# Moving the weight tiles of a decoder layer by 128 bytes and splitting its 512-column gate and up matmuls into 256-column ones

## The chip, the cores and the metric

The kernel runs on one core of a Trainium2 chip. The metric is the time of the program on the device, in microseconds; less is better. Before the change the runs took 1199.06 to 1200.92 us, median 1200.54. One further execution was profiled; it took 1200.04 us.

## The reference, cut to what matters

One decoder layer over 256 tokens of width 2048, in float32. An input projection feeds two groups of heads (a recurrent one, RWKV-7, and a latent attention), their outputs go through an output projection, and a gated MLP follows. The change touches the dense products around them; the core of the MLP is

```python
h = rms_norm(x, ffn_norm_g[l])
gate = h @ w_gate                       # 2048 x 5632
gate = causal_depthwise_conv(gate, width 3) + conv_b
x = x + (silu(gate) * (h @ w_up)) @ w_down
```

The input projection is `rms_norm(x) @ w_in`, 2048 by 4448; the latent attention adds `w_uq`, `w_ukv`, and `w_out` is 2048 by 2048. A row's normalising factor commutes with a product, so the kernel applies it after the product, when it evicts the result.

## The kernel before, in words

**Split products.** Every dense product is made of three float32r products, which together come near float32: a float32 matrix W is split into hi (rounded to float32r) and lo (the rest), an activation likewise, and the kernel sums hi·hi, hi·lo and lo·hi. `piece` (L125) loads 512 KB of weights into a tile `raw`, ScalarE writes `hi` (L133), VectorE writes `lo` (L134). There are three buffers each of `raw`, `hi` and `lo`, of 4 KB in a partition.

**Three ways to order a product.** In `prod_b` and `prod_c` the weights stand still in TensorE (one 128 by 128 block per load) and the activations stream past. An activation block holds hi and lo side by side, 2 times 256 tokens.

- `prod_b` (L162, used by the FFN's gate and up products alone) streams hi and lo together, 512 columns past a block of W's hi (L165), into a whole 512-column PSUM accumulator; then 256 columns past each block of W's lo (L168). The accumulator ends as two halves, which `joined` (L181) adds: a ScalarE copy (L182), a VectorE add (L183), a VectorE multiply by the row factors (L184).
- `prod_c` (L171, input projection and latent up projections) makes three matmuls of 256 columns into the same 256 columns: two on W's hi (L175, with the block loaded for each), one on W's lo (L178). `scaled` (L186) evicts it in one VectorE multiply (L187).
- `prod_a` (L190: value up projection, output projection, down projection) turns it round: activations stand still, 512 columns of weights stream past (L197 to L199).

**Stages.** Input projection with the activation tiles named x and most of the recurrent heads' work (to 272 us of the span), latent projections with tiles named cl and the heads' ends (to 342 us), output projection in two halves (to 462 us), then twice: gate and up products of a block of columns (24 and 20 blocks of 128 columns each; L964 to L988), and the down products on them (L993 to L1020). Each of the 44 blocks of gate and up takes two accumulators and four pieces of weights, a piece being 8 weight blocks: 176 pieces in all. The FFN's activation tiles, named z, are four buffers of the pool a8, the same four that x had. Queues are filled by a scheduler at build time; within an engine the order is then fixed.

**Where the tiles lie.** Pools and single tiles are laid out in a partition in the order in which they are first used: `pad` (8 floats), the four buffers of a8 (8 KB each), `pad2` (8 floats), and behind it everything else, the pools of hi, lo and of the 4 KB tiles (s4) among it. All buffers of a8, s4, hi and lo are whole multiples of 256 bytes long, and a matmul's operands start at multiples of 512 bytes in them. So two operands keep one distance modulo 256 whatever the buffer and the block. In the program as built, the a8 buffers start at byte 160 modulo 256, and s4, hi and lo at 96. Below, *distance* is the start of the streaming operand less the start of the standing one, modulo 256:

| products | streams | stands | columns | distance before |
|---|---|---|---|---|
| gate and up, L165 and L168 | z (a8) | hi, lo | 512, 256 | 64 |
| input projection, L175 and L178 | x (a8) | hi, lo | 256 | 64 |
| latent q and k, L175 and L178 | cl (s4) | hi, lo | 256 | 0 |
| down projection, L197 to L199 | hi, lo | hh, hl (s4) | 512 | 0 |
| output projection, first half | hi, lo | yhi, ylo (s4) | 512 | 0 |
| output projection, second half | hi, lo | yhi, ylo (a8) | 512 | 192 |
| last pieces of the down projection | wt (a8) | hh, hl (s4) | 512 | 64 |

Of the kernel before, what the change touches and what calls it, by code (L numbers as in the profile page):

```python
# [14 lines left out]
ALU = mybir.AluOpType  # L15
AX = mybir.AxisListType

P = 128
T = 256
# [35 lines left out]
def hybrid_layer(ctx: ExitStack, tc: tile.TileContext, a: dict, out: bass.AP):  # L55
    nc = tc.nc
    V, S, PE = nc.vector, nc.scalar, nc.tensor
# [8 lines left out]
    def nm(s):  # L66
        uid[0] += 1
        return f"{s}{uid[0]}"
# [3 lines left out]
    def s4(dt=F32, n="s4"):  # L72
        return sb.tile([P, 1024], dt, tag="s4", name=nm(n), bufs=NS4)
# [8 lines left out]
    def hl4(n):  # L82
        return a8(n).rearrange("p (k s) t -> p k s t", s=2)

    def t1(n, w=T, dt=F32):
        return sb.tile([P, 260], dt, tag="t1", name=nm(n), bufs=NT1)[:, :w]
# [7 lines left out]
    def mm(n="mm"):  # L94
        return ps.tile([P, 512], F32, tag="mm", name=nm(n), bufs=NMM)
# [4 lines left out]
    def at(n="at"):  # L100
        return ps.tile([P, 512], F32, tag="at", name=nm(n), bufs=NAT)

    def con(shape, n, dt=F32):
        return sb.tile(shape, dt, name=n, bufs=1)
# [2 lines left out]
    nc.gpsimd.memset(pad, 0.0)  # L107
    xT = a["xT"]
    xs_ = [hl4("x") for _ in range(4)]
    pad2 = con([P, 8], "pad2")  # L110
    nc.gpsimd.memset(pad2, 0.0)
    vec = con([P, NVEC], "vec")
    cst = con([P, NCST], "cst")
# [11 lines left out]
    def piece(src, dst=None, eng=None):  # L125
        raw = sb.tile([P, 1024], F32, tag="raw", name=nm("raw"), bufs=NRAW)
        last_w[0] = nc.sync.dma_start(raw, src).ins
        if dst is None:
            hi = sb.tile([P, 1024], F32R, tag="hi", name=nm("hi"), bufs=NHI)
            lo = sb.tile([P, 1024], F32R, tag="lo", name=nm("lo"), bufs=NLO)  # L130
        else:
            hi, lo = (dst.rearrange("p k t -> p (k t)")[:, q * 1024:(q + 1) * 1024] for q in range(2))
        S.copy(hi, raw)  # L133
        sub = (eng or V).tensor_tensor(lo, raw, hi.bitcast(F32), ALU.subtract).ins  # L134
        if eng is None:
            last_lo[0] = sub
        return hi, lo

    def xsplit(g):
        raw = s4(n="xraw").rearrange("p (k t) -> p k t", k=4)  # L140
        nc.sync.dma_start(raw, xT[:, g * 4:(g + 1) * 4, :])
        for j in range(4):
            k = g * 4 + j
            h = xs_[g][:, j, 0, :]
            S.activation(h, raw[:, j, :], AF.Copy, scale=vv("ag", k))
            last_x[0] = V.scalar_tensor_tensor(xs_[g][:, j, 1, :], raw[:, j, :], vv("ag", k),
                                               h.bitcast(F32), ALU.mult, ALU.subtract).ins
        return raw
# [5 lines left out]
    def flush(every=False):  # L154
        now = [f for n, f in pend if n == 0 or every]
        pend[:] = [(n - 1, f) for n, f in pend if n > 0 and not every]
        for f in now:
            f()
# [3 lines left out]
    def prod_b(acc, pieces, act, kt0, n, first, last):  # L162
        hi, lo = pieces
        for j in range(n):
            PE.matmul(acc, hi[:, j * P:(j + 1) * P], act(kt0 + j), start=first and j == 0, stop=False,  # L165
                      skip_group_check=True)
        for j in range(n):
            PE.matmul(acc[:, :T], lo[:, j * P:(j + 1) * P], act(kt0 + j)[:, 0, :], start=False,  # L168
                      stop=last and j == n - 1, skip_group_check=True)

    def prod_c(acc, pieces, act, kt0, n, first, last):  # L171
        hi, lo = pieces
        for j in range(n):
            for s in range(2):
                PE.matmul(acc[:, :T], hi[:, j * P:(j + 1) * P], act(kt0 + j)[:, s, :],  # L175
                          start=first and j == 0 and s == 0, stop=False)
        for j in range(n):
            PE.matmul(acc[:, :T], lo[:, j * P:(j + 1) * P], act(kt0 + j)[:, 0, :], start=False,  # L178
                      stop=last and j == n - 1)

    def joined(dst, acc, scale):  # L181
        S.copy(dst, acc[:, T:])  # L182
        V.tensor_tensor(dst, acc[:, :T], dst, ALU.add)  # L183
        V.tensor_tensor(dst, dst, scale, ALU.mult)  # L184

    def scaled(dst, acc, scale, rows=slice(0, P)):  # L186
        V.tensor_tensor(dst, acc[rows, :T], scale[rows], ALU.mult)  # L187


# [11 lines left out]
    x_hl = lambda k: xs_[k // 4][:, k % 4, :, :]  # L201

    def in_tile(i, pf=mm):
        acc = pf()
        for h in range(2):
            eng = nc.gpsimd if h and 17 <= i < 25 else None
            prod_c(acc, piece(a["win"][i, h], eng=eng), x_hl, h * 8, 8, h == 0, h == 1)
        flush()
        return acc

# [108 lines left out]
    acc0 = [mm(), mm(), at()]  # L319
    pcs = {}  # L320
# [10 lines left out]
    with tc.manual_schedule(engines={mybir.EngineType.SP}):  # L331
        for g in range(4):
            xsplit(g)
            if g == 0:
                nc.scalar.dma_start(cst, a["cst"])
            if g % 2 == 0:
                for i in range(2):
                    pcs[i, g // 2] = piece(a["win"][wt0[i], g // 2])
            for i in range(2):
                hl = tuple(u[:, (g % 2) * 512:(g % 2 + 1) * 512] for u in pcs[i, g // 2])  # L340
                prod_c(acc0[i], hl, x_hl, g * 4, 4, g == 0, g == 3)
        for h in range(2):
            prod_c(acc0[2], piece(a["win"][26, h]), x_hl, h * 8, 8, h == 0, h == 1)
        sums(0)
        kacc[0] = in_tile(1)
        dve0 = last_lo[0]
        sums(1)
        kacc[1] = in_tile(2, ch)
        rope_tables()
        lora = s4(n="lora")  # L350
        nc.sync.dma_start(lora, a["lora"])

    rsB = sb.tile([P, T], F32, tag="rsB", name="rsB", bufs=1)
# [30 lines left out]
    def shifted(acc, i, rows=slice(0, P), dst=None):  # L384
        h = t1("h", 257)
        nc.gpsimd.memset(h[rows, 0:1], 0.0)
        scaled(h[rows, 1:257], acc, rsB, rows)
        o = t1("sh") if dst is None else dst
        S.activation(o[rows], h[rows, 1:257], AF.Copy, scale=om_mu[rows, i:i + 1])
        V.scalar_tensor_tensor(o[rows], h[rows, 0:256], vv("mu", i, rows), o[rows], ALU.mult, ALU.add)  # L390
        return o
# [49 lines left out]

    acc = acc0[2]
    kraw, ksw = t1("kraw"), t1("ksw")
    scaled(kraw[0:64], acc, rsB, slice(0, 64))
    shifted(acc, 26, rows=slice(64, 96), dst=sg2)
    sigmoid_(sg2, slice(64, 96))
    nc.gpsimd.dma_start(kraw[64:128], kraw[0:64])
# [11 lines left out]
    for p in range(8):  # L459
        pp, g = p // 2, p % 2  # L460
# [3 lines left out]
        acc = kacc[p] if p in kacc else in_tile(1 + p)  # L464
# [45 lines left out]
    for p in range(8):  # L510
        pp, g = p // 2, p % 2
        acc = in_tile(9 + p)
# [254 lines left out]
    cl, rrs, rrB = [], [], []  # L767

    def latent(x, gname, post):
        c_ = [s4(F32R, "cl").rearrange("p (k s t) -> p k s t", k=2, s=2) for _ in range(2)]  # L770
        ssum = t2("css")
        for j in range(4):
            acc = in_tile(27 + x * 4 + j)
            cr = t2("cr")
            scaled(cr, acc, rsB)
            if j == 0:
                S.activation(ssum, cr, AF.Square)
            else:
                sq = t2("csq")
                S.activation(sq, cr, AF.Square)  # L780
                V.tensor_tensor(ssum, ssum, sq, ALU.add)
            h_, l_ = (c_[j // 2][:, j % 2, q, :] for q in range(2))
            S.activation(h_, cr, AF.Copy, scale=vv(gname, j))
            V.scalar_tensor_tensor(l_, cr, vv(gname, j), h_.bitcast(F32), ALU.mult, ALU.subtract)
        pss = at("pss")
        for tb in range(2):
            PE.matmul(pss[:, tb * 2:tb * 2 + 2], ssum[:, tb * P:(tb + 1) * P], ones[:, 0:2], start=True, stop=True)
        m = st("ssm", 2)
        V.tensor_copy(m, pss[:, 0:4:2])
        rr = con([P, 2], f"rr{x}")  # L790
        V.tensor_scalar(rr, rsqrt(m, 1.0 / 512, EPS, 2), post, None, ALU.mult)
        rb = con([P, T], f"rrB{x}")
        bcast(rr, rb, at, t2)
        rrs.append(rr)
        rrB.append(rb)
        cl.append(c_)
# [12 lines left out]
    def up_b(src, i, x, dsts):  # L809
        pcs = piece(src[i])  # L810
        for j in range(2):
            acc = mm()
            prod_c(acc, (pcs[0][:, j * 512:(j + 1) * 512], pcs[1][:, j * 512:(j + 1) * 512]),
                   lambda k: cl[x][k // 2][:, k % 2, :, :], 0, 4, True, True)
            scaled(dsts[j], acc, rrB[x])

    for i in range(4, 6):
        up_b(a["wuq"], i, 0, [qr[:, (i - 4) * 2 + j, :] for j in range(2)])
# [145 lines left out]
    for blk, nf in enumerate((24, 20)):  # L964
        hh = [s4(F32R, "hh").rearrange("p (k t) -> p k t", k=4) for _ in range(nf // 4)]
        hl = [s4(F32R, "hl").rearrange("p (k t) -> p k t", k=4) for _ in range(nf // 4)]
        for fi in range(nf):
            f = f0 + fi
            accs = []
            for gu in range(2):  # L970
                acc = mm()
# [24 lines left out]
        n = nf // 2  # L996
# [105 lines left out]
```

## Time and profile before

| | us |
|---|---|
| median of 3 runs | 1200.54 |
| the profiled execution | 1200.04 |
| its span, first to last instruction | 1198.3 |
| TensorE busy (PE) | 1164.2 |
| weight loads busy (PEld) | 1026.2 |
| VectorE busy (DVE) | 817.5 |
| ScalarE busy (ACT) | 582.9 |

The span is what the profile covers; 1.7 us of the execution lie around it. A matmul in the profile is two instructions, the load of the standing operand (PEld) and the matmul (PE), which overlap, and the recorded matmuls overlap each other too. So the pace of a stream of matmuls is read from the distance of two starts, not from the length of one. In the chain of waits, each line has the start in us, the length in us, the engine, the tile written, the line of the kernel, and how many were merged; along a stream of matmuls each of them is there from its own predecessor's end, so the length divided by the count is the pace.

### The profile page before, as it was taken

What the parts mean: (1) busy time and instruction counts of PE and PEld (TensorE: products, weight loads), DVE (VectorE), ACT (ScalarE), POOL (GpSimd) and SP (SyncE); (2) the same over time, 40 slices, a digit from 0 to 9 for tenths busy, and PEclk for the clock granted to TensorE, in tenths of its full rate; (3) what the DMA queues carried; (4) which work ended last, traced back from release to release, by engine and by line L of the source; (5) the groups of instructions that cost most, each with busy time, mean ns of one, the idle gap of its engine ahead of it and who ended that gap; (6) DMA issues with size and microseconds to landing.
All of it is one profiled execution on the core that took longest, in us unless ns stands there. A gap on an engine that the chain in (4) does not pass through costs nothing.

```text
span 1198.3 us, 19598 instructions
## 1 busy us (share of the span) xinstructions
PE 1164.2 (97%) x7633; PEld 1026.2 (86%) x7633; DVE 817.5 (68%) x1296; ACT 582.9 (49%) x883; POOL 77.3 (6%) x214
## 2 busy tenths in 40 slices
PE   7899998999999999999999999999999999999996
PEld 7899988998877888888888888888888888888885
DVE  6797549867986566777777775444577777775663
ACT  6674334433434455655555554333455555554542
POOL 1500232011110001000000000000000000000000
PEclk9999999989998999999999999999999999999999
DMA  8554454735233554655555555555655555566662
GB/s 325 169 156 162 133 155 140 226 106 181 89 124 124 184 182 165 205 193 187 189 191 190 194 193 187 189 197 190 204 191 191 187 191 191 193 219 213 202 217 81
DMA packets 71022, 215.90 MB, mean 180 GB/s; under 512 B 17616, under 2 KB 17872, under 8 KB 70928
## 3 DMA queue, kind: packets, MB, share of 16 engines
q1 hardware_dynamic: 69776, 211.84, 54.1%
q10 hardware_dynamic: 768, 2.05, 0.5%
q8 instruction: 60, 0.98, 0.3%
q0 software_dynamic: 384, 0.75, 0.3%
q14 instruction: 34, 0.28, 0.1%
HBM read 210.48 MB, written 3.41 MB: 179 GB/s over the span
## 4 chain that ended last, share of the span: by engine, by line
PE 91%; DVE 4%; DMA 2%; issue 1%; ACT 1%; SPq 1%; POOL 0%; ACTq 0%; POOLq 0%
PE mm L165 27%; PE mm L168 14%; PE mm L175 10%; PE mm L197 9%; PE mm L198 9%; PE mm L199 9%; PE mm L178 5%; PE pg L539 1%; PE px L689 1%; DVE Tq L596 1%; DMA xraw<-in_xT 1%; PE py L689 1%; DMA Lp<-dL 1%; DVE lo L134 0%; DMA xt<-in_x 0%
## 5 line engine op out<-in xcount | busy, mean ns | idle before, releaser
L134 DVE TENSOR_TENSOR lo<-raw,hi 128x1024 fp32r<-128x1024 f32 x368 | 450.3, 1224 | 274.5 <-ACT hi L133 271.0
L133 ACT CAST hi<-raw 128x1024 fp32r<-128x1024 f32 x376 | 394.7, 1050 | 477.0 <-issue 154.6
L165 PE MATMUL mm<-z,hi 128*128 128x512 f32 x1408 | 351.3, 392 | 0.0
L165 PEld LDWEIGHTS mm<-z,hi 128*128 128x128 f32 x1408 | 251.9, 188 | 43.7
L168 PEld LDWEIGHTS mm<-z,lo 128*128 128x128 f32 x1408 | 188.3, 188 | 14.5
L168 PE MATMUL mm<-z,lo 128*128 128x256 f32 x1408 | 191.6, 278 | 0.0
L175 PE MATMUL mm<-x,hi 128*128 128x256 f32 x1056 | 149.6, 289 | 11.6 <-ACT hi L133 8.2
L175 PEld LDWEIGHTS mm<-x,hi 128*128 128x128 f32 x1056 | 135.7, 194 | 14.5 <-ACT hi L133 8.2
L198 PE MATMUL mm<-lo,hh 128*128 128x512 f32 x336 | 130.7, 389 | 0.0
L199 PE MATMUL mm<-hi,hl 128*128 128x512 f32 x336 | 130.7, 389 | 0.0
L197 PE MATMUL mm<-hi,hh 128*128 128x512 f32 x336 | 119.7, 389 | 0.0
L178 PE MATMUL mm<-x,lo 128*128 128x256 f32 x528 | 77.2, 285 | 0.0
L199 PEld LDWEIGHTS mm<-hi,hl 128*128 128x128 f32 x336 | 63.1, 188 | 13.1
L197 PEld LDWEIGHTS mm<-hi,hh 128*128 128x128 f32 x336 | 63.1, 188 | 13.1
L198 PEld LDWEIGHTS mm<-lo,hh 128*128 128x128 f32 x336 | 63.1, 188 | 13.0
L178 PEld LDWEIGHTS mm<-x,lo 128*128 128x128 f32 x528 | 69.4, 193 | 0.1
L198 PE MATMUL mm<-lo,yhi 128*128 128x512 f32 x128 | 51.4, 402 | 0.0
L199 PE MATMUL mm<-hi,ylo 128*128 128x512 f32 x128 | 50.8, 397 | 0.0
L197 PE MATMUL mm<-hi,yhi 128*128 128x512 f32 x128 | 49.9, 409 | 0.0
L976 POOL MEMSET gt<- 128x2 f32 x44 | 4.3, 99 | 575.9 <-DVE hl L988 559.0
L199 PEld LDWEIGHTS mm<-hi,ylo 128*128 128x128 f32 x128 | 24.4, 190 | 5.3
L198 PEld LDWEIGHTS mm<-lo,yhi 128*128 128x128 f32 x128 | 24.4, 190 | 5.0
(277 smaller groups left out, 1111.0 us busy)
## 6 DMA issues: line engine op xcount, KB each, us to landing
raw<-in_wgu SPq DMA_DIRECT2D x176, 512.0 KB, 3.6
raw<-in_wdn SPq DMA_DIRECT2D x88, 512.0 KB, 4.2
raw<-in_win SPq DMA_DIRECT2D x70, 512.0 KB, 3.7
raw<-in_wout SPq DMA_DIRECT2D x32, 512.0 KB, 3.3
raw<-in_wuq SPq DMA_DIRECT2D x6, 512.0 KB, 3.3
xraw<-in_xT SPq DMA_DIRECT2D x4, 512.0 KB, 6.3
xt<-in_x SPq DMA_DIRECT2D x4, 512.0 KB, 6.9
raw<-in_wuv SPq DMA_DIRECT2D x4, 512.0 KB, 3.3
```

The costliest lines, as they stand in the source:

```text
L133: S.copy(hi, raw)
L134: sub = (eng or V).tensor_tensor(lo, raw, hi.bitcast(F32), ALU.subtract).ins
L165: PE.matmul(acc, hi[:, j * P:(j + 1) * P], act(kt0 + j), start=first and j == 0, stop=False, skip_group_check=True)
L168: PE.matmul(acc[:, :T], lo[:, j * P:(j + 1) * P], act(kt0 + j)[:, 0, :], start=False, stop=last and j == n - 1, skip_group_check=True)
L175: PE.matmul(acc[:, :T], hi[:, j * P:(j + 1) * P], act(kt0 + j)[:, s, :], start=first and j == 0 and s == 0, stop=False)
L178: PE.matmul(acc[:, :T], lo[:, j * P:(j + 1) * P], act(kt0 + j)[:, 0, :], start=False, stop=last and j == n - 1)
L197: PE.matmul(accs[tb], ah, wh, start=first and j == 0, stop=False)
L198: PE.matmul(accs[tb], ah, wl, start=False, stop=False)
L199: PE.matmul(accs[tb], al, wh, start=False, stop=last and j == n - 1)
L539: PE.matmul(pg[h][:, o:o + P], BK[pp][hs, gg, w * 2 + r, :, :], AR[pp][hs, gg, w * 2 + r, :, :], start=o == 0, stop=True, skip_group_check ...
L596: V.tensor_tensor(Tq[:, 0:n, i + 1:32], Tq[:, 0:n, i + 1:32], tv, ALU.add)
L689: PE.matmul(dst[HS[h], a_ * 64:(a_ + 1) * 64], lhsT, rhs, start=n == 0 and a_ == 0, stop=True, skip_group_check=True)
```

## The change

`pad2` gets 40 floats in place of 8, so everything behind it lies 128 bytes further on and the a8 buffers stay. `prod_c` takes the name `prod_b`, and the old `prod_b` goes; `scaled` takes the name `joined`, and the old three-step `joined` goes. So the FFN's gate and up products are made of three 256-column matmuls for each weight block, with one-step evictions, as the input projection's already were. All the other edits are these names.

```diff
-    pad2 = con([P, 8], "pad2")
+    pad2 = con([P, 40], "pad2")
...
     def prod_b(acc, pieces, act, kt0, n, first, last):
         hi, lo = pieces
         for j in range(n):
-            PE.matmul(acc, hi[:, j * P:(j + 1) * P], act(kt0 + j), start=first and j == 0, stop=False,
-                      skip_group_check=True)
-        for j in range(n):
-            PE.matmul(acc[:, :T], lo[:, j * P:(j + 1) * P], act(kt0 + j)[:, 0, :], start=False,
-                      stop=last and j == n - 1, skip_group_check=True)
-
-    def prod_c(acc, pieces, act, kt0, n, first, last):
-        hi, lo = pieces
-        for j in range(n):
             for s in range(2):
                 PE.matmul(acc[:, :T], hi[:, j * P:(j + 1) * P], act(kt0 + j)[:, s, :],
                           start=first and j == 0 and s == 0, stop=False)
...
-    def joined(dst, acc, scale):
-        S.copy(dst, acc[:, T:])
-        V.tensor_tensor(dst, acc[:, :T], dst, ALU.add)
-        V.tensor_tensor(dst, dst, scale, ALU.mult)
-
-    def scaled(dst, acc, scale, rows=slice(0, P)):
+    def joined(dst, acc, scale, rows=slice(0, P)):
         V.tensor_tensor(dst, acc[rows, :T], scale[rows], ALU.mult)
```

The distances become: gate and up 192, input projection 192, latent q and k 0, down projection 0, output projection 0 in the first half and 64 in the second, the last pieces of the down projection 192.

On TensorE, one accumulator of the FFN (two pieces) stood like this before, in the middle of the first 24 blocks; the names are accumulator, streaming tile, standing tile, and x4 is four in a row:

```order
L165 MATMUL mm_6037<-z_4913,hi_6040 128x512 x4
L165 MATMUL mm_6037<-z_4914,hi_6040 128x512 x4
L168 MATMUL mm_6037<-z_4913,lo_6041 128x256 x4
L168 MATMUL mm_6037<-z_4914,lo_6041 128x256 x4
L165 MATMUL mm_6037<-z_4915,hi_6062 128x512 x4
L165 MATMUL mm_6037<-z_4916,hi_6062 128x512 x4
L168 MATMUL mm_6037<-z_4915,lo_6063 128x256 x4
L168 MATMUL mm_6037<-z_4916,lo_6063 128x256 x4
```

With the change, the same place on TensorE:

```order
L166 MATMUL mm_6221<-z_4913,hi_6224 128x256 x8
L166 MATMUL mm_6221<-z_4914,hi_6224 128x256 x8
L169 MATMUL mm_6221<-z_4913,lo_6225 128x256 x4
L169 MATMUL mm_6221<-z_4914,lo_6225 128x256 x4
L166 MATMUL mm_6221<-z_4915,hi_6254 128x256 x8
L166 MATMUL mm_6221<-z_4916,hi_6254 128x256 x8
L169 MATMUL mm_6221<-z_4915,lo_6255 128x256 x4
L169 MATMUL mm_6221<-z_4916,lo_6255 128x256 x4
```

Each run of four 512-column matmuls is a run of eight 256-column ones now; the runs on lo stay. A piece has 24 matmuls and weight loads in place of 16; over the FFN that is 1408 of each more.

On VectorE, one block of the FFN before (gt and up are the evicted gate and up, cv the convolution, lo the split of the weights that come next):

```order
L183 TENSOR_TENSOR gt_7045<-mm_6955,gt_7045 128x256
L184 TENSOR_TENSOR gt_7045<-gt_7045,rs2B 128x256
L134 TENSOR_TENSOR lo_7088<-raw_7085,hi_7087 128x1024
L980 SCALAR_TENSOR_TENSOR cv_7050<-gt_7045,vec,cv_7050 128x256
L981 SCALAR_TENSOR_TENSOR cv_7050<-gt_7045,vec,cv_7050 128x256
L134 TENSOR_TENSOR lo_7111<-raw_7108,hi_7110 128x1024
L183 TENSOR_TENSOR up_7055<-mm_7000,up_7055 128x256
L184 TENSOR_TENSOR up_7055<-up_7055,rs2B 128x256
L985 TENSOR_TENSOR up_7055<-up_7055,cv_7050 128x256
L134 TENSOR_TENSOR lo_7133<-raw_7130,hi_7132 128x1024
L988 TENSOR_TENSOR hl_5347<-up_7055,hh_5341 128x256
```

With the change, the same block on VectorE:

```order
L174 TENSOR_TENSOR gt_7092<-mm_6970,rs2B 128x256
L134 TENSOR_TENSOR lo_7109<-raw_7106,hi_7108 128x1024
L967 SCALAR_TENSOR_TENSOR cv_7095<-gt_7092,vec,cv_7095 128x256
L968 SCALAR_TENSOR_TENSOR cv_7095<-gt_7092,vec,cv_7095 128x256
L134 TENSOR_TENSOR lo_7139<-raw_7136,hi_7138 128x1024
L174 TENSOR_TENSOR up_7100<-mm_7031,rs2B 128x256
L134 TENSOR_TENSOR lo_7170<-raw_7167,hi_7169 128x1024
L972 TENSOR_TENSOR up_7100<-up_7100,cv_7095 128x256
L134 TENSOR_TENSOR lo_7200<-raw_7197,hi_7199 128x1024
L975 TENSOR_TENSOR hl_5347<-up_7100,hh_5341 128x256
```

The add is gone from each of the two evictions, and ScalarE loses its two copies (L182) in the same way. Up to the start of the FFN the order on TensorE, VectorE and ScalarE is that of before, and SyncE's queue of transfers is the same throughout.

More of the change, by code (lines that the diff above doesn't have):

```diff
@@ L206, in in_tile @@
             eng = nc.gpsimd if h and 17 <= i < 25 else None
-            prod_c(acc, piece(a["win"][i, h], eng=eng), x_hl, h * 8, 8, h == 0, h == 1)
+            prod_b(acc, piece(a["win"][i, h], eng=eng), x_hl, h * 8, 8, h == 0, h == 1)
         flush()
@@ L340, in hybrid_layer @@
                 hl = tuple(u[:, (g % 2) * 512:(g % 2 + 1) * 512] for u in pcs[i, g // 2])
-                prod_c(acc0[i], hl, x_hl, g * 4, 4, g == 0, g == 3)
+                prod_b(acc0[i], hl, x_hl, g * 4, 4, g == 0, g == 3)
         for h in range(2):
-            prod_c(acc0[2], piece(a["win"][26, h]), x_hl, h * 8, 8, h == 0, h == 1)
+            prod_b(acc0[2], piece(a["win"][26, h]), x_hl, h * 8, 8, h == 0, h == 1)
         sums(0)
@@ L386, in shifted @@
         nc.gpsimd.memset(h[rows, 0:1], 0.0)
-        scaled(h[rows, 1:257], acc, rsB, rows)
+        joined(h[rows, 1:257], acc, rsB, rows)
         o = t1("sh") if dst is None else dst
@@ L443, in hybrid_layer @@
     kraw, ksw = t1("kraw"), t1("ksw")
-    scaled(kraw[0:64], acc, rsB, slice(0, 64))
+    joined(kraw[0:64], acc, rsB, slice(0, 64))
     shifted(acc, 26, rows=slice(64, 96), dst=sg2)
@@ L774, in latent @@
             cr = t2("cr")
-            scaled(cr, acc, rsB)
+            joined(cr, acc, rsB)
             if j == 0:
@@ L812, in up_b @@
             acc = mm()
-            prod_c(acc, (pcs[0][:, j * 512:(j + 1) * 512], pcs[1][:, j * 512:(j + 1) * 512]),
+            prod_b(acc, (pcs[0][:, j * 512:(j + 1) * 512], pcs[1][:, j * 512:(j + 1) * 512]),
                    lambda k: cl[x][k // 2][:, k % 2, :, :], 0, 4, True, True)
-            scaled(dsts[j], acc, rrB[x])
+            joined(dsts[j], acc, rrB[x])
     for i in range(4, 6):
```

## The prediction

> **What bounds the kernel now.** I read the page first, then the chain of waits in each stage. From the page: the span, the engines, and the chain by line.
>
> ```profile
> span 1198.3 us, 19598 instructions
> PE 1164.2 (97%) x7633; PEld 1026.2 (86%) x7633; DVE 817.5 (68%) x1296; ACT 582.9 (49%) x883; POOL 77.3 (6%) x214
> PE 91%; DVE 4%; DMA 2%; issue 1%; ACT 1%; SPq 1%; POOL 0%; ACTq 0%; POOLq 0%
> PE mm L165 27%; PE mm L168 14%; PE mm L175 10%; PE mm L197 9%; PE mm L198 9%; PE mm L199 9%; PE mm L178 5%; PE pg L539 1%; PE px L689 1%; DVE Tq L596 1%; DMA xraw<-in_xT 1%; PE py L689 1%; DMA Lp<-dL 1%; DVE lo L134 0%; DMA xt<-in_x 0%
> ```
>
> TensorE is the chain for 91% of the span, and 41% are the two lines of gate and up. Next the stretches: the FFN's first gate and up, and the input projection.
>
> ```profile
> 500.00:700.00 200.00, 200.00 (x1162) 176.09 (x1161) 146.39 (x218) 105.58 (x163) 1.89 (x19) 1.00 0.58 191
> 208.00:231.00 23.00, 23.00 (x198) 23.00 (x197) 20.27 (x42) 12.54 (x19) 0.00 (x0) 1.00 0.68 222
> ```
>
> Columns are the stretch, PE, PEld, DVE, ACT, POOL, granted clock, DMA share, GB/s. In the FFN, TensorE is busy all 200 us at full clock, VectorE 146, ScalarE 106, the DMA engines 0.58: nothing but TensorE limits it. So the pace of one matmul after another is what the change is worth, and the chain gives it. FFN, eight matmuls to a row:
>
> ```profile
> 479.24 0.91 PE mm L168 x8
> 480.14 1.83 PE mm L165 x8
> 481.97 0.94 PE mm L168 x8
> 482.92 1.83 PE mm L165 x8
> 484.75 0.91 PE mm L168 x8
> 485.66 1.83 PE mm L165 x8
> ```
>
> A 512-column matmul takes 1.83 / 8 = 229 ns. The 256-column ones come in two paces, in turn: 0.91 / 8 = 114 ns and 0.94 / 8 = 117.5 ns, same line, same shape, same distance of 64. The pace therefore isn't fixed by the shape. A piece is 2.74 or 2.77 us, 2.755 on average (479.24 to 481.97 and 481.97 to 484.75 are one of each).
>
> Now the same pace elsewhere. Input projection (256 columns, distance 64), then latent projections (256 columns, distance 0):
>
> ```profile
> 216.61 1.88 PE mm L175 x16
> 218.49 0.94 PE mm L178 x8
> 219.43 1.88 PE mm L175 x16
> 221.32 0.94 PE mm L178 x8
> ...
> 333.69 0.96 PE mm L175 x8
> 334.65 0.48 PE mm L178 x4
> ```
>
> The input projection takes 4.71 us for the 40 matmuls from 216.61 to 221.32, 117.8 ns each, and it stays there: the slower of the FFN's two paces, which I take at 117.8 too. The latent ones take (0.96 + 0.48) / 12 = 120 ns. And the 512-column ones, in the down projection (distance 0) and the output projection's second half (distance 192):
>
> ```profile
> 750.03 0.45 PE mm L197 x2
> ...
> 752.75 0.45 PE mm L197 x2
> ...
> 416.89 0.24 PE mm L197
> 417.12 0.23 PE mm L198
> 417.35 0.24 PE mm L199
> 417.59 0.23 PE mm L197
> 417.82 0.24 PE mm L198
> 418.06 0.23 PE mm L199
> 418.29 0.24 PE mm L197
> ```
>
> From 750.03 to 752.75 lie 12 matmuls: 226.7 ns each. From 416.89 to 418.29 lie six: 233.3 ns each. So with the streaming operand at distance 0, 64 and 192 from the standing one, 512 columns take 226.7, 229 and 233.3 ns; 256 columns take 120 at distance 0 and 114 or 117.8 at 64. Half of 226.7 is 113.3, which is the faster of the FFN's 256-column paces within the rows' rounding: I take it that 0.443 ns a column is the stream undisturbed (113.3 and 226.7), and the rest, 0 to 7 ns for each weight load, is the stream meeting the load of the next weights in the memory.
>
> The Trainium skill speaks against that reading: "TensorE: Matmul & The Clock Gate", section "Step-by-step: what each phase is for", has two independent read ports and says that loading the next weights takes no bandwidth from the running matmul. By that rule a shift of 128 bytes changes no pace. The rows of 114, 117.8 and 120 ns for one shape at one clock do not agree with it, unless something else than the address makes them; what it would give is the first rival below.
>
> **The change part by part.**
>
> Gate and up. Each of the 176 pieces has 24 matmuls of 256 columns in place of 8 of 512 and 8 of 256. Its price depends on the pace at distance 192 with 256 columns, which no row shows. The bounds: from below 113.3 ns, since no stream here goes under 0.443 ns a column; from above 120 ns by the slowest 256-column row, or, with what a 512-column load loses at 192 (233.3 − 226.7 = 6.6), 113.3 + 6.6 = 119.9, the same. Which value? The two widths order the distances in opposite ways: 512 columns lose 0 at distance 0, 2.3 at 64, 6.6 at 192, while 256 columns lose 6.7 at 0 and half as much at 64 (0 or 4.5). A 256-column matmul ends about when the load of the next weights does (PEld 23.00 of 23.00 us in the input projection, 176 of 200 in the FFN), so its stream and the load meet at another place in the pattern than in a 512-column one, and the losses fall along 0, 64 where those of the wide ones rise. Carried on to 192 that is no loss: 113.3 ns. This is a continuation over two points, not a proof, and the chance below says so. The sum: 24 × 113.3 = 2.720 us against 2.755, 35 ns a piece, 176 pieces, **−6.2 us**. At 120 ns it would be 2.880, +0.125 × 176 = +22.0 us.
>
> Input projection. The same matmuls on the same buffers, so the same pace: from 117.8 to 113.3, 4.5 ns each. Not all of them are on the path. In these rows stand the matmuls of L175 by stretch, and under them those of L178:
>
> ```profile
> 42.00:158.00 116.00, 70.22 (x496) 62.99 (x496) 0.99 0.47 146
> 195.00:272.00 77.00, 44.88 (x317) 40.98 (x315) 0.93 0.53 160
> 42.00:158.00 116.00, 34.26 (x241) 30.89 (x241) 0.99 0.47 146
> 195.00:272.00 77.00, 23.05 (x156) 21.20 (x157) 0.93 0.53 160
> ```
>
> Before 42 us the chain runs through transfers and the split of the weights, and from 158 to 195 us through the solve of the recurrent heads:
>
> ```profile
> 33.09 4.58 DMA raw<-in_win
> ...
> 167.12 6.14 DMA Lp<-dL
> 176.09 2.09 DVE Tq L596
> ```
>
> What is left on TensorE's path is 496 + 317 + 241 + 156 = 1210 matmuls: 1210 × 4.5 = **−5.4 us**. At 120 ns it is +2.7. What the rest gains there, TensorE waits for the transfers and the solve instead.
>
> Output projection, second half: its 192 matmuls (four column blocks, four pieces, twelve each) go from distance 192 to 64, so from 233.3 to 229 ns: 192 × 4.3 = **−0.8 us**. The last pieces of the down projection go the other way, 48 matmuls from 64 to 192: **+0.2 us**. Latent, first half and down projection keep distance 0 and their pace.
>
> Evictions. Of each of 88, ScalarE loses the copy and VectorE the add:
>
> ```profile
> L183 DVE TENSOR_TENSOR up<-mm,up 128x256 f32<-128x256 f32 x44 | 18.4, 418 | 0.0
> L182 ACT COPY gt<-mm 128x256 f32<-128x256 f32 x44 | 16.2, 367 | 0.0
> L165 PE MATMUL mm<-z,hi 128*128 128x512 f32 x1408 | 351.3, 392 | 0.0
> ```
>
> That is 88 × 0.42 = 37 us of VectorE and 88 × 0.36 = 32 us of ScalarE, all beside TensorE, which waits 0.0 us before L165: worth nothing now. They also leave more room for the splits of weights, so if a piece is 1% shorter, those still keep up: VectorE falls from 73% to about 66% of a piece, ScalarE from 53 to about 47%, and 191 GB/s become 193 with the DMA engines at 0.58. Were that cover gone, an eviction of 0.37 and 0.42 us and a multiply of that size, about 1.2 us, would stand open for each accumulator; there are three buffers for them, and two are in use.
>
> Sum: −6.2 − 5.4 − 0.8 + 0.2 = −12.2 us. The profiled execution's 1200.0 becomes 1187.8; it lies 0.5 under the median of the runs, so **1188 us**.
>
> **The rivals.**
>
> *The distance does nothing, and 256 columns cost what they cost in the input projection.* There the weight load is busy 23.00 of 23.00 us: the load of 128 columns and its hand-over would be the limit, not the stream, and 117.8 ns holds wherever every matmul is 256 wide. For it: the input projection's steady pace on the very buffers that z uses. Against: eight loads in a row at 114 ns in every other piece of the FFN. Time: 24 × 117.8 = 2.827 us a piece, +0.072 × 176 = +12.7 us, nothing elsewhere: 1213 us. It decides from 114.8 ns up (2.755 / 24), where the FFN gains nothing by the split. This is also what the Trainium skill's two ports would give.
>
> *Distance 192 costs 256 columns what it costs 512.* 6.6 ns a load, 120 ns: +22.0 in the FFN, +2.7 in the input projection, −0.6 from the two small groups: 1224 us. For it: the only rows at 192 are the slowest of the wide ones. Against: distance 0 is the best for wide ones and the worst for narrow ones, so rows of one width don't carry over.
>
> *Both paces stay, in turn.* As in L168 now, pieces fall into 114 or 117.8 according to how the one before ended, on average 115.6 ns: FFN +3.4, input projection −2.7, small groups −0.6: 1200 us, no change.
>
> **How the numbers follow.** The forecast has 0.58, the first rival (1213) 0.18, the second (1224) 0.16, the third (1200) 0.08. The forecast's own range is 1184 to 1193: at its low end the matmuls of the input projection that I left out count too (−2), and the stages' uneven beginnings gain as much again; at its high end the input projection gives nothing. The range to hold the time 8 times in 10 takes in the third and the first rival, 1184 to 1214, and leaves out the second and some of the forecast's tails: 0.16 and 0.04. A difference of 0.2%, 2.4 us, is about what a measurement here tells from none. Faster is the forecast and a quarter of the third rival: 0.60; same is most of what is left of that: 0.05; slower are the first two and the rest: 0.35.
>
> **What would show it.** In the chain of the changed kernel, rows of L166 with 16 matmuls in the FFN should read 1.81 us and rows of L169 with 8 should read 0.91, all alike; 1.88 and 0.94 would be the first rival, 1.92 and 0.96 the second. The input projection should show the same, with its gain seen only outside the first 42 us and the solve, whose transfers and steps should end no earlier than the matmuls before them let them. The output projection's second half should go from 233 to 229 ns. TensorE's wait before L166 in the FFN should stay at 0; if a wait for hi or lo shows there, the splits of weights have become late and the cover was thinner than I think. The prediction is wrong if the FFN's pieces take over 2.755 us.

## The result, and the profile after

The changed kernel took 1210.2 us (median of 6 runs, 1207.2 to 1215.5) against 1200.9 for the kernel before (6 runs): a ratio of 1.0084, with a 95% interval of 1.0067 to 1.0102. It is slower, by about 10 us. The page of the changed kernel's profiled execution (1210.41 us):

```profile
span 1208.6 us, 22236 instructions
PE 1173.0 (97%) x9041; PEld 1093.6 (90%) x9041; DVE 776.7 (64%) x1208; ACT 564.5 (47%) x795; POOL 76.2 (6%) x214
PE 88%; DVE 5%; DMA 3%; issue 1%; ACT 1%; POOL 0%; SPq 0%; ACTq 0%; POOLq 0%
PE mm L166 36%; PE mm L169 18%; PE mm L184 9%; PE mm L186 9%; PE mm L185 9%; DMA raw<-in_win 2%; DVE Tq L583 1%; DVE lo L134 1%; PE px L676 1%; PE pg L526 1%; DVE tm L581 1%; PE py L676 1%; DMA Lp<-dL 0%; DMA dT<-Tq 0%; ACT hi L133 0%
```

There are 1408 more matmuls, VectorE has 41 us less to do and ScalarE 18 us less, and TensorE is the chain as before. Where the stages begin in the two traces (first matmul of each, in us):

| stage | before | after | length before | length after |
|---|---|---|---|---|
| up to the FFN | 0 | 0 | 462.0 | 459.9 |
| gate and up, 24 blocks | 462.0 | 459.9 | 266.1 | 272.5 |
| down | 728.1 | 732.4 | 130.6 | 130.5 |
| gate and up, 20 blocks | 858.7 | 862.9 | 220.6 | 226.2 |
| down, and the end | 1079.3 | 1089.1 | 119.0 | 119.5 |

So the loss is in gate and up, +6.4 and +5.6 us, and 2.1 us are won before it. The chain of waits in the changed kernel's first gate and up stage, 16 matmuls on hi or 8 on lo to a row:

```profile
478.13 1.89 PE mm L166 x16
480.01 0.94 PE mm L169 x8
```

These are 117.8 ns a matmul, hi and lo alike, and it stays so to the end of both stages. A piece is 2.83 us against 2.755 before. But the same shape at the same distance of 192 has another pace in the input projection of the same execution:

```profile
85.46 1.59 PE mm L166 x13
87.05 0.91 PE mm L169 x8
87.96 1.81 PE mm L166 x16
89.77 0.34 PE ssP L459 x4
90.11 1.05 PE mm L169 x8
91.16 1.89 PE mm L166 x16
93.05 0.94 PE mm L169 x8
```

From 87.05 to 89.77 us 113 ns each; then four small float32 matmuls of the recurrent heads come in between, and behind them the same product goes on at 117.8. Of the input projection's matmuls, 62% ran at 113.3 here; at distance 64, in the trace of before, 4%.

The FFN's first stage has such a change near its start too. It begins at 117.8, float32 transposes of 128 columns (`pxT`) come in between, and behind them it runs at 113.3. Then the broadcast of the row factors (`rsb`, float32 matmuls of 128 columns) comes in:

```profile
467.29 2.38 PE mm L166 x21
469.67 0.44 PE rsb L227 x4
470.12 1.65 PE mm L166 x14
```

That is 113.3 ns ahead of the broadcast and 117.9 behind it. Nothing else comes into the stage after that, and the remaining 262 us of it run at 117.8. The second stage starts at 117.8 straight from the down products, with nothing in between.

The input projection gave the theory that I took to the experiments. **Two self-holding paces:** a stream of 256-column matmuls, each with its weight load, has a pace of 113.3 ns and one of 117.8 ns, it stays in the one that it is in for as long as nothing else comes between, and a different matmul in between (a 512-column one, a small float32 one) can throw it from one to the other. The distance decides which paces exist and which is fallen into more often. Both stages of the FFN were at 117.8 when the last thing that could disturb them had passed. **Rivals:** the weight load sets 117.8 for any stream that is 256 wide throughout, whatever the address; and the pace is a function of the distance alone.

### The profile page after: what moved, and what is told of

It is laid out like the page before. It is cut to its first block, busy times and chain, and to the rows that moved or that the text cites. A ratio compares the mean times of both kernels' runs of the same rounds, so it can differ in the third digit from the quotient of the medians.

```text
span 1208.6 us, 22236 instructions
## 1 busy us (share of the span) xinstructions
PE 1173.0 (97%) x9041; PEld 1093.6 (90%) x9041; DVE 776.7 (64%) x1208; ACT 564.5 (47%) x795; POOL 76.2 (6%) x214
## 4 chain that ended last, share of the span: by engine, by line
PE 88%; DVE 5%; DMA 3%; issue 1%; ACT 1%; POOL 0%; SPq 0%; ACTq 0%; POOLq 0%
PE mm L166 36%; PE mm L169 18%; PE mm L184 9%; PE mm L186 9%; PE mm L185 9%; DMA raw<-in_win 2%; DVE Tq L583 1%; DVE lo L134 1%; PE px L676 1%; PE pg L526 1%; DVE tm L581 1%; PE py L676 1%; DMA Lp<-dL 0%; DMA dT<-Tq 0%; ACT hi L133 0%
## 5 line engine op out<-in xcount | busy, mean ns | idle before, releaser
L166 PE MATMUL mm<-z,hi 128*128 128x256 f32 x2816 | 361.5, 281 | 0.0
L166 PEld LDWEIGHTS mm<-z,hi 128*128 128x128 f32 x2816 | 344.4, 189 | 0.2
L169 PE MATMUL mm<-z,lo 128*128 128x256 f32 x1408 | 195.0, 281 | 0.0
L169 PEld LDWEIGHTS mm<-z,lo 128*128 128x128 f32 x1408 | 179.0, 189 | 0.0
L166 PE MATMUL mm<-x,hi 128*128 128x256 f32 x1056 | 148.3, 289 | 13.7 <-ACT hi L133 8.4
L166 PEld LDWEIGHTS mm<-x,hi 128*128 128x128 f32 x1056 | 134.7, 196 | 16.6 <-ACT hi L133 8.4
L174 DVE TENSOR_TENSOR up<-mm,rs2B 128x256 f32<-128x256 f32 x44 | 18.7, 424 | 59.1 <-PE mm L169 59.1
L174 DVE TENSOR_TENSOR gt<-mm,rs2B 128x256 f32<-128x256 f32 x44 | 18.7, 425 | 46.3 <-PE mm L169 46.3
```

## The experiments

The time is the median of several runs with the ratio to the kernel before and its 95% interval. "Stages" are the two gate and up stages of the profiled execution; before they took 266.1 and 220.6 us, with the change 272.5 and 226.2.

| run | distance of x and z | gate and up | stages, us | time, us | ratio |
|---|---|---|---|---|---|
| mix192 | 192 | 512 and 256 | 267.7, 221.9 | 1202.4 | 1.0017 (1.0004 to 1.0031) |
| split64 | 64 | 256 | 272.7, 226.1 | 1211.2 | 1.0097 (1.0077 to 1.0117) |
| mix0 | 0 | 512 and 256 | 269.4, 223.4 | 1207.9 | 1.0074 (1.0059 to 1.0089) |
| split0 | 0 | 256 | 277.8, 230.4 | 1222.1 | 1.0186 (1.0171 to 1.0201) |
| split128 | 128 | 256 | 277.7, 230.4 | 1221.1 | 1.017 (1.015 to 1.019) |
| mix128 | 128 | 512 and 256 | 271.1, 224.8 | 1210.8 | 1.0074 (1.006 to 1.0089) |
| kick192 | 192 | 256, one wide block a stage | 263.3, 218.7 | 1191.9 | 0.9923 (0.9908 to 0.9937) |
| reroll192 | 192 | 256, 44 small matmuls | 268.8, 222.9 | 1202.5, one run | |
| roll2 | 192 | 256, 2 small matmuls | 263.5, 218.4 | 1193.5 | 0.9947 (0.9928 to 0.9966) |
| evict3 | 192 | as kick192, long evictions | 263.3, 218.7 | 1191.8 | 0.9937 (0.9917 to 0.9957) |
| kick64 | 64 | 256, one wide block a stage | 272.4, 218.6 | 1203.8 | 1.0034 (1.0019 to 1.0049) |
| kick64odd | 64 | 256, one wide piece a stage | 263.3, 226.1 | 1201.9 | 1.0021 (1.001 to 1.0031) |

### Each half of the change alone

The move alone, in the kernel before (mix192):

```diff
-    pad2 = con([P, 8], "pad2")
+    pad2 = con([P, 40], "pad2")
```

> The weight tiles 128 bytes further on alone (distance 192), gate and up as before in 512 and 256 columns. All theories: the 512-column matmuls of gate and up go from 229 to about 233.3 ns, the pace that 512 columns had at distance 192, +6.1 us. Theory of two self-holding paces: the input projection runs at 113.3 in some stretches and 117.8 in others, as in the changed kernel, and the runs of eight on lo fall into one or the other after each 512-column run; together 1200 to 1207 us. Theory that the weight load sets 117.8 whatever the address: the input projection stays at 117.8 and the time is about 1206 us.

The chain in its first gate and up stage:

```profile
601.79 1.86 PE mm L165 x8
603.65 0.91 PE mm L168 x8
```

The 512-column matmuls take 232.7 ns on average, as expected, and cost 5.2 us over 1408. The runs on lo, half of which ran at 117.8 before, fall to 113.3 in 173 of the 176 pieces (0.91 for eight): −2.4 us. The stages are 1.6 and 1.3 us longer, and the whole ends at 1202.4. In the input projection about 60% of the matmuls ran at 113.3, where the theory that the weight load sets the pace expected 117.8 throughout. So the move alone is nearly even, and 192 is where a stream is thrown into the quicker pace after a 512-column matmul.

The split alone, in the changed kernel (split64):

```diff
-    pad2 = con([P, 40], "pad2")
+    pad2 = con([P, 8], "pad2")
```

> The split into 256 columns alone, with the weight tiles where they were (distance 64). Two self-holding paces: each of the FFN's two gate and up stages keeps one pace throughout, 113.3 (2.72 us a piece) or 117.8 (2.83 us); 1194 us for both fast, 1213 for both slow, about 1204 for one of each. Weight load sets the pace: 117.8 in both stages, 1213 us. Pace fixed by the distance: 117.8 from the input projection's rows at 64, 1213 us.

```profile
502.50 1.88 PE mm L166 x16
504.38 0.94 PE mm L169 x8
```

117.8 ns throughout both stages, 1211.2 us: the slower of the two paces in both, which all three theories allow. The split alone carries the whole loss, and the distance makes no difference to it here.

### Other distances

The same line for both forms, mix0 and mix128 from the kernel before, split0 and split128 from the changed one; 24 floats give distance 0, and 56 in their place give 128:

```diff
-    pad2 = con([P, 8], "pad2")
+    pad2 = con([P, 24], "pad2")
```

> The weight tiles 64 bytes further on (distance 0 for gate and up and the input projection), otherwise the kernel before. The 512-column matmuls of gate and up should fall from 229 to 226.7 ns, the down projection's pace at distance 0: -3.2 us. Pace fixed by the distance: all 256-column ones at 120 ns as the latent ones at distance 0, +6.1 us for the runs on lo and +2.7 in the input projection, 1206 us. Two self-holding paces: the runs on lo may hold 113.3 after the steady 226.7, then 1194 to 1200 us. Weight load sets the pace: 117.8 to 120 everywhere, 1203 to 1206 us.

> The split into 256 columns with the weight tiles 64 bytes further on (distance 0). Pace fixed by the distance, and also two self-holding paces if distance 0 has only the slow one: 120 ns everywhere, a piece 2.88 us, 1225 us. Weight load sets the pace regardless of the address: 117.8, 1213 us.

> The split with the weight tiles 192 bytes further on (distance 128). Two self-holding paces: the distance sets which paces exist, 120 alone at 0, 113.3 and 117.8 at 64 and 192; at 128 not known: 2.72 to 2.88 us a piece, 1192 to 1225 us. Weight load sets the pace: 117.8, 1211 us; but 120 at distance 0 already spoke against one pace for all.

> The kernel before with the weight tiles 192 bytes further on (distance 128). The 512-column matmuls are not known at 128; the wide ones took 226.7 to 230 at 0, 229 at 64 and 233 at 192, so 226.7 to 236. If 256 columns hold 113.3 there, the input projection gains 5 us; 1190 to 1210 us.

The first row is of split0, the next of split128:

```profile
500.94 1.92 PE mm L166 x16
502.86 0.96 PE mm L169 x8
```

```profile
603.06 1.92 PE mm L166 x16
604.98 0.96 PE mm L169 x8
```

At 0 and at 128, gate and up run at 120.0 ns; at 0, no stretch of the input projection reached 113.3 either. That fells the rival of one pace for any address: the same instructions take 120 at another distance. (That the load doesn't need 117.8 either is seen where the same load goes at 113.3, in the input projection above and in kick192 below.) At 128 the input projection averaged 118.8, so 120 is not the only pace there. In mix0 the 512-column matmuls did not keep the 226.7 ns that I expected: they took 230.0 on average. Behind each run on lo (119.1) the first five of a run on hi average 228 to 236, and only the last three are at 226.7, as in the long undisturbed runs of the down projection. My forecast of 1194 to 1200 us from the two paces missed there. mix128 has 232.7 and 118.6. Neither distance is any use.

The edit to `pad2` moves the weights' own address as well as the distance. The products whose two operands move together tell these apart: in all fourteen traces, with the weights at four places modulo 256, the latent q and k products average 119.5 to 119.6 ns and the down products 226.7 to 226.8. So it is the distance that counts, and not the weights' address alone.

### Throwing the stream into the other pace

If the pace is held and not given, one disturbance at the right place is worth a whole stage. kick192 is the changed kernel with one block of each stage in the old form (`prod_w` and `joined_w` are the kernel before's `prod_b` and three-step `joined`):

```diff
-                    prod_b(acc, piece(a["wgu"][f, gu, h]), z_hl, h * 8, 8, h == 0, h == 1)
+                    (prod_w if fi == 2 else prod_b)(acc, piece(a["wgu"][f, gu, h]), z_hl, h * 8, 8, h == 0, h == 1)
...
-            joined(gt[:, 2:258], accs[0], rs2B)
+            (joined_w if fi == 2 else joined)(gt[:, 2:258], accs[0], rs2B)
...
-            joined(up, accs[1], rs2B)
+            (joined_w if fi == 2 else joined)(up, accs[1], rs2B)
```

> The changed kernel, but in each of the two gate and up stages the third block alone (fi == 2) has the kernel before's 512 and 256 columns and three-step eviction. Two self-holding paces: that block ends in a run of eight on lo that fell to 113.3 after a 512-column one, as all of them did at distance 192 in the run with the weight tiles moved alone, and the 84 and 68 pieces behind it keep that pace to the end of the stage: 2.72 in place of 2.83 us, about -16 us, 1193 to 1195 us, and under the kernel before. Weight load sets the pace, or the distance alone does: the pieces behind the wide block run at 117.8 as before it, 1210 us.

The chain around that block (L176 and L179 are the wide block's), and the last rows of the same stage:

```profile
477.96 1.53 PE mm L166 x13
479.49 0.94 PE mm L169 x8
480.43 1.86 PE mm L176 x8
482.30 0.92 PE mm L179 x8
...
488.77 1.86 PE mm L176 x8
490.63 0.91 PE mm L179 x8
491.54 1.81 PE mm L166 x16
493.35 0.91 PE mm L169 x8
...
717.30 1.81 PE mm L166 x16
719.11 0.91 PE mm L169 x8
```

Ahead of the block 117.8 ns, behind it 113.3 to the end, 228 us later, both at a granted clock of 1.00. The second stage does the same. The stages are 9.2 and 7.5 us shorter than with the change, and the kernel takes 1191.9 us, a little under the expected 1193: it beats both the kernel before and the changed one. Distance, shape and evictions of these pieces are those of the changed kernel, so none of them fixes the pace.

Is it the wide block as such? reroll192 puts one float32 matmul of two columns, which reads that block's evicted `up`, into each of the 44 blocks; its result is not used:

```diff
+            PE.matmul(ch("rk")[:, 0:2], ident, up[:, 0:2], start=True, stop=True)
             hv = hh[fi // 4][:, fi % 4, :]
```

> The changed kernel with one float32 matmul of two columns put into TensorE's queue in every one of the 44 blocks; its result is not used. Two self-holding paces: the pace changes only at these matmuls, within a few matmuls of them, and is one of 113.3 and 117.8 all the way to the next; some blocks run at 113.3. Each costs about 0.1 to 0.3 us of its own. Weight load or distance alone: 117.8 in all blocks.

```profile
506.48 0.91 PE mm L169 x8
507.38 1.59 PE mm L166 x14
508.97 0.12 PE rk L973 x2
509.09 0.34 PE mm L166 x2
509.43 0.92 PE mm L169 x8
510.35 1.81 PE mm L166 x16
```

Behind each such matmul the next few of the stream are slower, then all run at 113.3 to the next. About 90% of the matmuls on hi have the quicker pace. The first such matmul of each stage came upon a stream at 117.8; the other 40 came upon 113.3 and left it so. Each costs: 0.34 us for two matmuls behind it where 0.23 would do, and 0.12 of its own. So two are better than 44 (roll2):

```diff
+            if fi == 1 - blk:
+                PE.matmul(ch("rk")[:, 0:2], ident, up[:, 0:2], start=True, stop=True)
```

> The changed kernel with one float32 matmul of two columns in each of the two gate and up stages (its result is not used), in TensorE's queue behind the first few blocks. Two self-holding paces: behind it 113.3 ns to the end of the stage, as behind each of the 42 seen; without the cost of the other 42 (about 0.25 us each), 1190 to 1193 us, as with the wide block. If instead the wide block's gain came from something else it brought, such as its eviction or its place in the order, 1210 us.

1193.5 us, half a microsecond above the expected range, the stages 263.5 and 218.4 us; the rows behind the small matmul read 1.81 and 0.91. A matmul with no use at all wins as much as the wide block, whose shape and evictions are therefore not what the gain needs. And the evictions, in kick192 (evict3):

```diff
+    def joined_3(dst, acc, scale):
+        S.copy(dst, acc[:, :T])
+        V.tensor_scalar(dst, dst, 1.0, 1.0, ALU.mult, ALU.mult)
+        V.tensor_tensor(dst, dst, scale, ALU.mult)
...
-            (joined_w if fi == 2 else joined)(gt[:, 2:258], accs[0], rs2B)
+            (joined_w if fi == 2 else joined_3)(gt[:, 2:258], accs[0], rs2B)
...
-            (joined_w if fi == 2 else joined)(up, accs[1], rs2B)
+            (joined_w if fi == 2 else joined_3)(up, accs[1], rs2B)
```

> The kernel with one wide block per stage, but all other gate and up evictions made in three steps again (a ScalarE copy, a VectorE multiply by one, the VectorE multiply by the row factors), so that ScalarE and VectorE carry what they did before. The evictions are beside TensorE, so the time stays at that of the kernel with the wide block, 1192 us, within 2 us. If the one-step evictions carried part of the gain, it gives up to 10 us back.

1191.8 us, with VectorE at 806 us and ScalarE at 583, near what they carried before. The one-step evictions are worth nothing that can be measured.

### The same at distance 64

kick64 is kick192 with `pad2` at 8 floats (first two lines); kick64odd has a single wide piece in place of four besides (the rest):

```diff
-    pad2 = con([P, 40], "pad2")
+    pad2 = con([P, 8], "pad2")
...
-                    (prod_w if fi == 2 else prod_b)(acc, piece(a["wgu"][f, gu, h]), z_hl, h * 8, 8, h == 0, h == 1)
+                    (prod_w if fi == 2 and gu == 0 and h == 0 else prod_b)(acc, piece(a["wgu"][f, gu, h]), z_hl, h * 8, 8, h == 0, h == 1)
...
-            (joined_w if fi == 2 else joined)(up, accs[1], rs2B)
+            joined(up, accs[1], rs2B)
```

> The wide third block with the weight tiles where they were (distance 64): four wide pieces. There the run on lo was fast and slow in turn, piece by piece. Two self-holding paces, entered at the slow one: wide pieces one and three end fast, two and four slow, so behind the block the stage goes on at 117.8, about 1211 us. If a wide block as such frees the stream, 1195 us.

> The same at distance 64 with a single wide piece (the first half of the third block's gate). Two self-holding paces, entered at the slow one: the single wide piece ends in a fast run on lo, and the stage goes on at 113.3 behind it, about 1194 us. If distance 64 cannot hold 113.3 over a long run of 256-column matmuls, 1211 us as with four wide pieces.

The first fence is kick64's first stage, the second kick64odd's first, the third kick64odd's second stage (behind its wide piece):

```profile
486.27 1.83 PE mm L176 x8
488.10 0.91 PE mm L179 x8
489.01 1.83 PE mm L176 x8
490.84 0.94 PE mm L179 x8
...
494.52 1.83 PE mm L176 x8
496.35 0.94 PE mm L179 x8
497.29 1.88 PE mm L166 x16
499.18 0.94 PE mm L169 x8
```

```profile
485.36 1.83 PE mm L176 x8
487.19 0.91 PE mm L179 x8
488.10 1.81 PE mm L166 x16
489.91 0.91 PE mm L169 x8
```

```profile
880.73 1.88 PE mm L166 x16
882.61 0.94 PE mm L169 x8
```

The first stages came out as expected, piece by piece: four wide pieces end at 117.8 and the stage stays there (272.4 us), one ends at 113.3 and the stage stays there (263.3). So distance 64 holds 113.3 too, over 230 us. In the second stages it was the other way round: four pieces ended quick (218.6 us), one slow (226.1). Yet ahead of the wide pieces the stream ran at 117.8 in all four stages. What differed was the first wide matmul, 229 ns in the first stages and 235 in the second. So the state that the stream is in holds more than the pace, and what else it holds isn't shown. My expected times, 1211 and 1194, missed that, and both kernels came out at one stage of each, 1203.8 and 1201.9 us, where 1204 had been expected for one of each under split64. At 64 the two paces alone don't tell how a wide piece ends; at 192 all 16 wide pieces of kick192 and evict3 and all 44 two-column matmuls within the stages ended at 113.3, and so did 173 of the 176 pieces of mix192.

## Why the prediction was wrong, point by point

- **What bounds the kernel: right.** TensorE's pace decides, the evictions nothing (evict3), and no wait appeared ahead of L166 in the FFN.
- **The two bounds: right.** No stretch of 256-column matmuls held a pace under 113.3 ns in any trace (kick192 stays on it), and 120 is the slowest steady one (split0, split128).
- **Gate and up, −6.2 us: the step that failed.** The prediction took the pace at distance 192 as one number and carried it on from two points, "Carried on to 192 that is no loss: 113.3 ns". At 192 there are two paces, and the distance alone doesn't choose. The stages ran at 117.8 ns: +12.0 us in place of −6.2. The price of the quick pace was right: with one wide block kept, the two stages are 4.7 us shorter than before, against 6.2 for all pieces from the first.
- **What the prediction had in its hands.** It showed the runs on lo at 114 and 117.5 in turn, for one line, shape and distance, and said that the pace isn't fixed by the shape. The same rows say that it isn't fixed by the distance either, and the 40 matmuls in a row at 117.8 say that it holds. The third rival came nearest in kind, pieces at one pace or the other "according to how the one before ended", but took it for an average; in a stage that nothing disturbs it is all or nothing: 1192 us with both stages quick, 1210 with both slow.
- **The first rival's time, 1213, was near, and its mechanism wrong.** Neither is 117.8 what the load needs (113.3 in kick192), nor does the distance do nothing (120.0 in split0). It came near because both stages happened to be left at 117.8; with one wide block ahead the same kernel takes 1192. Its page, the Trainium skill's "TensorE: Matmul & The Clock Gate", section "Step-by-step: what each phase is for", has loading the next weights take no bandwidth from the running matmul. By that the distance should change nothing. The runs differ: moving one operand by 64 bytes takes the steady pace from 117.8 (split64) to 120.0 ns (split0), and the measurement decides; that the load is what slows the stream is not shown.
- **The second rival, 120 at 192, is out.** No stream at 192 ran at it.
- **Input projection, −5.4, and output projection, −0.8, against 2.1 us together.** Partly the pace: 62% at 113.3, not all (49 to 64% in the six traces at 192). Partly cover: the solve of the recurrent heads, which I had on the path from 158 to 195 us, now ends later than TensorE's own work up to 235 us. The chain's first long stream also began 2.2 us later, behind a transfer of 6.58 us in place of 4.58. In the changed kernel's chain:

```profile
222.03 1.21 DVE lo L134
...
223.65 5.24 DMA dT<-Tq
...
229.27 4.68 DMA T<-dU
```

  In the trace of before, TensorE's input projection stood on the chain there. The start of the FFN also varies: 456.5 to 461.5 us in the six traces at distance 192 (after, mix192, kick192, reroll192, roll2, evict3), whose instructions up to there are the same, and 461.2 to 462.2 in the four at 64. On average that is 2.8 us gained. At 192 the spread goes with the granted clock, which the sum left out. Each trace has stretches at a granted clock of 0.50 before the FFN: 13.7 us of them in kick192 (456.5), 20.5 in roll2, reroll192 and evict3 (457.9 to 459.2), 23.9 in the changed kernel (459.9), 27.3 in mix192 (461.5). The trace of before has 20.5 as well, so against the three that match it the gain is 2.8 to 4.1 us, not 2.1. Both terms together were still sized too large, at 6.2.
- **The small terms: right.** The output projection's second half went from 233.1 to 229.2 ns, the last pieces of the down projection from 229.2 to 233.3. For 512 columns in a long run the distance does fix the pace; that is why the step from there to 256 columns looked safe.

What the runs don't settle is what the two paces are inside the memory or the array. That the stream and the load of the next weights meet in some pattern of 256 bytes fits the distances, but it is argued, not shown; no run separated the two reads. Why the row factors' broadcast throws the stream to 117.8 where a two-column matmul throws it to 113.3 is open too. The broadcast did so in all five traces at 192 with the split (after, kick192, reroll192, roll2, evict3). Only one execution of the changed kernel was profiled, so whether others fall otherwise was not seen; but its six times, 1207.2 to 1215.5 us, go in the order of their mean granted clocks, 0.991 to 0.983, and so need no other cause.

## What to carry to other kernels

Read the pace of a dense stream from the distance of starts, and in more than one place: if one shape has two paces in one trace, find out what it did just before, since the pace can be a state that holds and not a price per instruction. Where a long stream sits in the slower one, a single different matmul ahead of it may be worth more than the edit under study: 16 to 18 us here for one wide block or one two-column matmul a stage. It can go the other way as well: here the row factors' broadcast put the first stage into the slower pace. So look at the pace behind each such matmul. A sum over instructions with a price taken from another stage is only safe if that stage is entered in the same way.

## What the runs showed of the hardware that I had not expected

- In the FFN, float32r matmuls of 256 columns with a 128-column weight load each hold 113.3 or 117.8 ns (distances 64 and 192 modulo 256) or 120.0 ns (0 and 128) over 200 us without a change.
- At distance 192 a float32 matmul of two columns (two each in reroll192 and roll2), or one run of 512-column ones (kick192, evict3), moved such a stream from 117.8 to 113.3 within a few matmuls. Other float32 ones went both ways: transposes of 128 columns near the FFN's start from 117.8 to 113.3, the broadcast of the row factors (128 columns) right behind them from 113.3 to 117.8, in each of five traces. At distance 64 both left it at 117.8 (split64, kick64, kick64odd).
- 512-column ones in the same kind of stream settle at 226.7 ns at distance 0 (down projection), and take 229 at 64 and 233 at 192 on average.
